# Two transformer blocks on one core: another order of ScalarE's steps in each expert, both gather halves evicted together, and the steps between router and first expert rearranged

## The chip, the cores and the metric

The kernel runs on one core of one Trainium2 chip. The metric is the device time of one execution in microseconds (us), start to end. PE is TensorE (matmuls), DVE is VectorE, ACT is ScalarE, POOL is GpSimd, SP is SyncE, which issues the loads of weights.

## The reference

A batch of one sequence of 256 tokens with 1024 features goes through two blocks in float32. The first block is a mixer (sliding-window attention with sinks, 8 heads of 64, beside gated linear attention), and then a mixture of 32 experts, of which each token takes its 4 best:

```
    logits = (h @ w_router).astype(jnp.float32) + b_router.astype(jnp.float32)
    top_v, top_i = lax.top_k(logits, TOP_K)
    gates = jax.nn.softmax(top_v, axis=-1)
...
        u = xb @ w_mlp1[e] + b_mlp1[e]
        x_glu = jnp.minimum(u[..., ::2], SWIGLU_LIMIT)
        x_lin = jnp.clip(u[..., 1::2], -SWIGLU_LIMIT, SWIGLU_LIMIT)
        a = x_glu * jax.nn.sigmoid(SWIGLU_ALPHA * x_glu) * (x_lin + 1)
        return a @ w_mlp2[e] + b_mlp2[e]
```

An expert goes from 1024 features to 2048 and, through `a` of 1024, back to 1024; a token's four results are added with their gates as weights.

The second block is a feed-forward part (2816 wide), a mixer of block attention (8 heads of 64) and spatial gating, and a second feed-forward part. All weights come from HBM once; the experts' are 384 MB.

## The kernel before

**Weights.** Every weight matrix is cut into chunks of 1 MB. `load_more` issues them on SP's queue in the order of use; a chunk is issued when the buffer that it takes has been released (`done`). In the expert stage there are 20 such buffers. An expert has 12 chunks: eight of `w_mlp1` (`m1`, k = 0 to 7) and four of `w_mlp2` (`m2`). They are released in fours: `m1` 0 to 3 after the branch at L1604, `m1` 4 to 7 after the branch at L1655, the `m2` four after the branch at L1672. All instructions stand in the order in which the code is written (`manual_schedule`), engine by engine.

**Router.** After the mixer, PE transposes the token rows and computes the router's logits (`pl`); DVE finds the four best, their one-hot rows `oh` and the counts `M`; PE makes positions from `M` (`pp`), DVE makes the selection `sel` of the first two experts. `x_hi` and `x_lo` are the rounded high part and the rest of the token rows: ACT copies `x_hi` (L1347), POOL subtracts `x_lo` (L1348).

**Gather.** Two experts are a group of 128 slots. `gather_rows` multiplies `sel` with `x_hi` and `x_lo` into two banks of 512 features, `gather_half` evicts one bank to `xr` on ACT (scaled by `yg`), PE transposes it four times into the same bank, and ACT and DVE take turns to write `xg`, features by slots, of both experts. There is one buffer `xr`, so the second eviction waits until the first half is transposed. The gather of the next group stands in the odd expert of a group, between the matmuls of that expert.

**An expert.** `up_start` writes the biases into two banks `u`; `up` multiplies `xg` with the eight `m1` chunks, of which the first half of the outputs (bank `u0`) ends earlier than the second. `glu` is four DVE steps and one ACT sigmoid `s` for each half and gives `a_sb`. Then comes the branch at L1655 (`more > 0`: the expert has over 64 tokens), `turn` (two transposes and ACT's copy to `aT`), the slot rows `pm`, and `down_q` over the four `m2` chunks into `yp`; before its second chunk the second half is turned. `rows_out` evicts `yp` (`yh`, `yl`), and `spread` adds it to the output banks `o_ps` during the next expert. `aT` has one buffer and shares it with `vx` of the branch. Before, the code reads:

```
            glu(us, a_sb, (0, 1))
            ax = P.tile([128, 1, 256], F32, name="ax", tag="sely", bufs=1)
            with tc.If(more > 0):
                nc.vector.tensor_tensor(vx, vx, up_more(range(4, KD)), op=OP.add)
                glu([vx], ax)
            ...
            pt = wps("apt")
            turn(a_sb, (0,), aT, pt)
```

**Attention.** `Attention.step` computes the scores of one pair of heads: for each head a matmul of 256 keys, one of 128 and the mask. A head has 64 features, so that the first head's matmuls use rows 0 to 63 of the array and the second's rows 64 to 127. There are four such steps in each block.

Of the kernel before, what the change touches and what calls it, by code (L numbers as in the profile page):

```python
# [10 lines left out]
F32 = mybir.dt.float32  # L11
# [4 lines left out]
AF = mybir.ActivationFunctionType  # L16
OP = mybir.AluOpType
# [7 lines left out]
CAP = 64  # L25
MORE = 32
# [20 lines left out]
def body(ctx: ExitStack, tc: tile.TileContext, I, out, dbg=None, n_experts=NE):  # L47
# [489 lines left out]
    class Attention:  # L537
# [8 lines left out]
        def step(self, i):  # L546
            pool, qT, kT = self.pool, self.qT, self.kT(i)
            ps = [self.bank("sc0"), self.bank("sc1")]
            for s in range(2):
                r = slice(64 * s, 64 * s + 64)  # L550
                nc.tensor.matmul(ps[s][:, 128:384], qT[r, i, 128:256], kT[r, :], start=True, stop=False,  # L551
                                 skip_group_check=True)
                nc.tensor.matmul(ps[s][:, 0:128], qT[r, i, 0:128], kT[r, 0:128], start=False, stop=False,
                                 skip_group_check=True)
                nc.tensor.matmul(ps[s][:, 0:384], ident_b, self.mask, start=False, stop=True, skip_group_check=True)
            yield
            S = pool.tile([128, 2, 384], F32, name="S", tag="S", bufs=2)
# [646 lines left out]
    with ExitStack() as ph:  # L1204
# [12 lines left out]
                                        qsl(b).to_broadcast([128, n, w]), op=OP.is_equal)  # L1217
            return sel

        def gather_rows(sel, w):  # L1220

            ps = []
            for q in range(2):
                p = wps("xrp")
                if q == 0:
                    for b in range(2):
                        nc.tensor.matmul(p[0:w, 0:1], sel[:, b].bitcast(F32), yt[:, b:b + 1], start=(b == 0),
                                         stop=(b == 1), skip_group_check=True)
                    yg = P.tile([128, 1], F32, name="yg", tag="yg", bufs=2)
                    nc.vector.tensor_copy(yg[0:w, :], p[0:w, 0:1])  # L1230
                    ps.append(yg)
                    first = p
                else:
                    for n, pn in ((1, p), (0, first)):
                        for b in range(2):
                            for x in (x_hi, x_lo):
                                nc.tensor.matmul(pn[0:w, :], sel[:, b], x[:, b, n * 512:(n + 1) * 512],  # L1237
                                                 start=(b == 0 and x is x_hi), stop=(b == 1 and x is x_lo),
                                                 skip_group_check=True)
                    ps += [p, first]  # L1240
            return ps

        def gather_half(ps, q, w, xgs):

            yg, p = ps[0], ps[1 + q]
            q = 1 - q
            xr = P.tile([128, 512], F32, name="xr", tag="yh", bufs=1)
            nc.scalar.activation(xr[0:w, :], p[0:w, :], AF.Copy, scale=yg[0:w, :])  # L1248
            for c in range(4):
                nc.tensor.transpose(p[:, c * w:(c + 1) * w], xr[0:w, c * 128:(c + 1) * 128], ident[0:w, 0:w])  # L1250
            for i, xg in enumerate(xgs):
                for c in range(4):
                    k = 4 * q + c
                    at = p[:, c * w + i * CAP:c * w + (i + 1) * CAP]
                    if c < 2:
                        nc.scalar.activation(xg[:, k, :], at, AF.Identity, scale=gs[:, 2, k:k + 1],  # L1256
                                             bias=modT[:, 24 + k:25 + k])
                    elif c == 2:
                        v = xg[:, k:k + 2, :]
                        at = p[:, c * w:4 * w].rearrange("p (c s) -> p c s", c=2)[:, :, i * CAP:(i + 1) * CAP]  # L1260
# [56 lines left out]

        x1 = xpool.tile([128, KD, T], F32, name="x1", tag="xb")
        pts = [acc("ht") for _ in range(4)]
        pl = wps("pl")  # L1320
        for h in range(2):
            for b in range(2):
# [16 lines left out]
                             stop=(b == 1), skip_group_check=True)  # L1339
        dump("x1T", x1)  # L1340

        x_hi = xpool.tile([128, 2, D], F32R, name="x_hi", tag="xb")
        x_lo = P.tile([128, 2, D], F32R, name="x_lo")
        for h in (1, 0):
            for b in range(2):
                cs = slice(h * 512, (h + 1) * 512)
                nc.scalar.activation(x_hi[:, b, cs], x_tok[:, b, cs], AF.Copy)  # L1347
                nc.gpsimd.tensor_tensor(x_lo[:, b, cs], x_tok[:, b, cs], x_hi[:, b, cs].bitcast(F32), op=OP.subtract)  # L1348
        slots.append((xpool, "xa", state["moe_end"] - 14))
        rt = P.tile([128, 2, NE], F32, name="rt", tag="aT")  # L1350
        for b in range(2):
            nc.vector.scalar_tensor_tensor(rt[:, b, :], pl[:, b * 32:(b + 1) * 32], yt[:, b:b + 1], lbias,
# [14 lines left out]
        for b in range(2):  # L1367
            with nc.allow_low_precision(reason="zeros and ones"):
# [11 lines left out]
        nc.vector.tensor_scalar(nit, pp[:, 64:96], float(MORE - 1 - CAP), None, op0=OP.add)  # L1380
        nc.vector.tensor_scalar(nit, nit, MORE.bit_length() - 1, None, op0=OP.arith_shift_right)
        nc.vector.tensor_scalar(nit, nit, 0.0, None, op0=OP.max)

# [4 lines left out]
        xg0 = group_tile(0)  # L1388
        w = group_size(0) * CAP
        xrs = gather_rows(sel0, w)  # L1390
        for h in range(2):
            gather_half(xrs, h, w, xg0)
        cur = sel0, xg0
# [12 lines left out]
        SW.close()  # L1406
        MW = ph.enter_context(ExitStack())
        banks["w"] = MW.enter_context(tc.tile_pool(name="psM", bufs=1, space=bass.MemoryType.PSUM))
        banks["tags"] = ["w0", "w1"]

        o_ps = [acc("moe_o") for _ in range(4)]
        for p in o_ps:

            nc.tensor.matmul(p, oh3[96:128, 0:1].to_broadcast([32, 128]), b13[96:128, 0:512], start=True, stop=False,
                             skip_group_check=True, tile_position=(96, 0))

        def o_part(b, dh, n):

            m = D // n
# [16 lines left out]
        def blocks(us, w):  # L1436
            n = 128 // w
            return [(us[i // n][w * (i % n):w * (i % n) + w, :], i, w * (i % n)) for i in range(4)]

        def up_start(us, w, e):  # L1440
            for u, i, c in blocks(us, w):
                nc.tensor.matmul(u, oh3[:, e:e + 1].to_broadcast([128, w]), b13[:, i * 512:(i + 1) * 512], start=True,
                                 stop=False, skip_group_check=True, tile_position=(0, c))

        def glu(us, a_sb, rs=(0,)):
            for r in rs:
# [117 lines left out]
        for e in range(n_experts):  # L1564
# [2 lines left out]
            sel, xg = cur  # L1567
            if look:
                nsel = group_select(gi + 1)
            us = [banks["w"].tile([128, 512], F32, name=f"u{i}", tag=f"u{i}") for i in range(2)]  # L1570

            def up(i, ks, us=us, xg=xg, e=e, j=j):
                for k in ks:
# [4 lines left out]
            up_start(us, CAP, e)  # L1578
            for k in range(3):
                up(0, (k,))  # L1580
                up(1, (k,))
# [26 lines left out]
                done(("m1", e, k))  # L1608
            if look:
                w = group_size(gi + 1) * CAP  # L1610
                xrs = gather_rows(nsel, w)
                nxg = group_tile(gi + 1)
                ahead = nsel, nxg

# [35 lines left out]
            a_sb = P.tile([128, 2, 256], F32, name="a_sb", tag="yl", bufs=1)  # L1650
            tg = P.tile([128, 2], F32, name="tg", tag="tg", bufs=1)
            sg = P.tile([128, T], F32R, name="sg", tag="sg", bufs=1)
            glu(us, a_sb, (0, 1))
            ax = P.tile([128, 1, 256], F32, name="ax", tag="sely", bufs=1)
            with tc.If(more > 0):  # L1655
                nc.vector.tensor_tensor(vx, vx, up_more(range(4, KD)), op=OP.add)
# [3 lines left out]
                done(("m1", e, k))  # L1660
            pt = wps("apt")
            turn(a_sb, (0,), aT, pt)
            pm = banks["w"].tile([128, 512], F32, name="pm", tag="u0")
            slots_of(e, sel[:, :, j], CAP, pm)
            slot_rows(pm, tg, sg)
# [397 lines left out]
```

## Time and profile before

| | us |
|---|---|
| median of 3 runs | 1793.35 (1787.22 to 1801.39) |
| the profiled execution | 1790.39 |
| its span, first to last instruction | 1788.7 |
| PE busy in the span | 1631.0 (91%) |
| DVE busy | 682.5 (38%) |
| ACT busy | 521.6 (29%) |

The experts' matmuls with `m1` chunks begin at 199.30 us of the span, and the last one with an `m2` chunk ends at 1202.0; the second block takes the rest. An expert takes from 26.4 to 50.6 us. The granted clock of TensorE is 0.969 of full over the span.

### The profile page before, as it was taken

How to read it: one execution, taken by the hardware profiler on the slowest of the kernel's cores; microseconds unless marked ns; L12 is line 12 of the kernel's file. 1: busy time of each engine (PE TensorE's matmuls, PEld its weight loads, DVE VectorE, ACT ScalarE, POOL GpSimd, SP SyncE). 2: the span in 40 equal slices, each digit the busy share in tenths (PEclk: the TensorE clock that was granted, in tenths of full speed). 3: DMA queues.
4: the chain of work that ended last, by engine and by line, in shares of the span. 5: the costliest groups of instructions: out<-in, count | busy, mean ns of one | idle time of the engine just before them, and what ended most of it. 6: DMA issues, size and time to landing. Idle time of an engine off the chain costs nothing. (4 is left out here: it accounts for less than half of the span.)

```text
span 1788.7 us, 25600 instructions
## 1 busy us (share of the span) xinstructions
PE 1631.0 (91%) x10067; PEld 996.7 (56%) x10067; DVE 682.5 (38%) x1424; ACT 521.6 (29%) x983; POOL 27.1 (2%) x43
## 2 busy tenths in 40 slices
PE   6998799999898798998989898888999999999997
PEld 3876333333333233333333333338999998999997
DVE  4656311211212112122121212217666775666666
ACT  2544211111011011111011111126444555554444
POOL 1000100000000000000000000100000000000000
PEclk8999899999899999999999999998999999999999
DMA  9987699799999999969999999973656653446552
GB/s 319 372 259 310 263 413 399 274 401 414 410 375 413 413 358 415 415 265 414 411 413 416 413 416 413 416 277 119 200 168 198 196 170 119 155 141 211 176 178 95
DMA packets 169755, 545.69 MB, mean 305 GB/s; under 512 B 11280, under 2 KB 90720, under 8 KB 133728
## 3 DMA queue, kind: packets, MB, share of 16 engines
q1 hardware_dynamic: 168304, 540.60, 79.0%
q8 instruction: 130, 2.13, 0.5%
q0 software_dynamic: 480, 1.58, 0.3%
q10 hardware_dynamic: 784, 0.92, 0.2%
q14 instruction: 57, 0.47, 0.1%
HBM read 542.01 MB, written 1.05 MB: 304 GB/s over the span
## 5 line engine op out<-in xcount | busy, mean ns | idle before, releaser
L1575 PE MATMUL u<-chunk,xg 128*64 128x512 f32 x2048 | 473.4, 604 | 2.7 <-PEq L1604 2.4
L1575 PEld LDWEIGHTS u<-chunk,xg 128*64 128x64 f32 x2048 | 156.2, 138 | 256.4 <-issue 247.0
L1477 PE MATMUL yp<-chunk,aT 128*64 128x512 f32 x1024 | 252.0, 636 | 48.4 <-ACT aT L1462 48.4
L448 DVE TENSOR_TENSOR ul<-chunk,uh 128x1024 fp32r<-128x1024 f32 x202 | 239.1, 1219 | 37.6 <-ACT uh L434 37.4
L434 ACT ACTIVATE uh<-chunk 128x1024 fp32r<-128x1024 f32 x202 | 205.2, 1049 | 59.5 <-DMA chunk<-in_ffn_w_up_dram 26.4
L310 PE MATMUL gu<-nhi,uh 128*128 128x256 f32 x704 | 200.1, 284 | 0.0
L310 PE MATMUL gu<-nhi,ul 128*128 128x256 f32 x704 | 199.4, 283 | 0.0
L310 PE MATMUL gu<-nlo,uh 128*128 128x256 f32 x704 | 199.4, 283 | 0.0
L1477 PEld LDWEIGHTS yp<-chunk,aT 128*64 128x64 f32 x1024 | 70.5, 143 | 174.3 <-issue 122.0
L310 PEld LDWEIGHTS gu<-nhi,uh 128*128 128x128 f32 x704 | 135.4, 192 | 1.2 <-issue 0.4
L310 PEld LDWEIGHTS gu<-nlo,uh 128*128 128x128 f32 x704 | 135.4, 192 | 0.9
L310 PEld LDWEIGHTS gu<-nhi,ul 128*128 128x128 f32 x704 | 135.4, 192 | 0.0
L1487 DVE SCALAR_TENSOR_TENSOR yl<-yp,tg,yh 128x512 fp32r<-128x512 f32 x32 | 24.0, 751 | 285.4 <-ACTq L1604 217.2
L1453 ACT ACTIVATE s<-g 128x256 f32<-128x256 f32 x66 | 27.5, 417 | 293.1 <-DVE g L1452 290.6
L1452 DVE TENSOR_SCALAR g<-u 128x256 f32<-128x256 f32 x64 | 27.1, 423 | 214.6 <-PE u L1575 212.8
L1486 ACT ACTIVATE yh<-yp,tg 128x512 fp32r<-128x512 f32 x32 | 22.0, 687 | 167.3 <-PEq L1672 150.4
L1248 ACT ACTIVATE xr<-xrp,yg 128x512 f32<-128x512 f32 x32 | 22.0, 686 | 145.1 <-PE xrp L1237 145.1
L1256 ACT ACTIVATE xg<-xrp,modT,gs 128x64 f32<-128x64 f32 x128 | 44.7, 399 | 64.6 <-PE xrp L1250 53.1
L1261 DVE TENSOR_TENSOR xg<-xrp,gs 128x128 f32<-128x128 f32 x64 | 18.7, 292 | 116.6 <-ACT xg L1256 116.6
L1142 DVE TENSOR_TENSOR gu<-gu,rs 128x512 f32<-128x512 f32 (+1 forms) x46 | 30.7, 667 | 80.7 <-PE gu L310 80.3
L1462 ACT ACTIVATE aT<-apt 128x256 f32<-128x256 f32 x64 | 24.5, 383 | 125.7 <-PE apt L297 93.6
L297 PEld LDWEIGHTS apt<-ident,a_sb 128*128 128x128 f32 x128 | 13.8, 149 | 77.9 <-issue 55.8
(472 smaller groups left out, 2402.4 us busy)
## 6 DMA issues: line engine op xcount, KB each, us to landing
chunk<-in_w_mlp_dram SPq DMA_DIRECT2D x384, 1024.0 KB, 9.5
chunk<-in_w_ada_dram SPq DMA_DIRECT2D x24, 1024.0 KB, 7.3
chunk<-in_ffn_w_gate_dram SPq DMA_DIRECT2D x22, 1024.0 KB, 5.4
chunk<-in_ffn_w_up_dram SPq DMA_DIRECT2D x22, 1024.0 KB, 7.9
chunk<-in_ffn_w_down_dram SPq DMA_DIRECT2D x22, 1024.0 KB, 5.8
chunk<-in_w_in_dram SPq DMA_DIRECT2D x17, 1024.0 KB, 5.2
chunk<-in_w_gate_dram SPq DMA_DIRECT2D x8, 1024.0 KB, 5.2
chunk<-in_w_out_dram SPq DMA_DIRECT2D x6, 1024.0 KB, 8.1
```

The lines of the kernel that those rows point to most:

```text
L310: nc.tensor.matmul(ps, a, b, start=first, stop=False, skip_group_check=True)
L434: nc.scalar.activation(hi if spec is None else spec(hi), view(raw(key)), AF.Copy)
L448: nc.vector.tensor_tensor(vl, view(raw(key)), vh.bitcast(F32), op=OP.subtract)
L1142: nc.vector.tensor_tensor(gu[:, a0:a1, :], p, rs[:, None, :].to_broadcast([128, a1 - a0, T]), op=OP.mult)
L1248: nc.scalar.activation(xr[0:w, :], p[0:w, :], AF.Copy, scale=yg[0:w, :])
L1256: nc.scalar.activation(xg[:, k, :], at, AF.Identity, scale=gs[:, 2, k:k + 1], bias=modT[:, 24 + k:25 + k])
L1452: nc.vector.tensor_scalar(g, uv[:, :, 0], 7.0, None, op0=OP.min)
L1453: nc.scalar.activation(s, g, AF.Sigmoid, scale=1.702)
L1462: nc.scalar.activation(aT[:, r * 256:(r + 1) * 256], pt[:, r * 256:(r + 1) * 256], AF.Copy)
L1477: nc.tensor.matmul(yp[w * d:w * d + w, 0:m], a, wt[:, o:o + m], start=(q + h == 0), stop=(q + h == 4), skip_group_check=True, tile_positio ...
L1487: nc.vector.scalar_tensor_tensor(yl, yp[:, 0:m], tg[:, 1:2], yh.bitcast(F32), op0=OP.mult, op1=OP.subtract)
L1575: nc.tensor.matmul(u, xg[j][:, k, :], raw(("m1", e, k))[:, n * 512:(n + 1) * 512], start=False, stop=(k == KD - 1), skip_group_check=True, ...
```

## The change

- In an expert the second half's `glu` stands behind the branch and behind the first half's `turn`. On ACT the order is sigmoid, copy to `aT`, sigmoid, copy, where it was two sigmoids and two copies.
- The gather evicts both banks one after the other (`gather_out`, two buffers `xr`), then transposes both; features 0 to 511 come first, and the `x_hi` matmuls of a bank stand ahead of its `x_lo` ones.
- `x_lo` is computed by DVE, after `yg` of the first group, where POOL computed it after each part of `x_hi`.
- The matmuls that open the output banks `o_ps` with zeros and the first expert's biases (`up_start`) stand ahead of the router's `pp`; the banks are laid out earlier for it. Four small DVE steps (`nit`, `nmax`, `q3`) move behind the first gather.
- The scores of a pair of heads alternate between the heads.

```
-            for s in range(2):
-                r = slice(64 * s, 64 * s + 64)
+            for s, r in enumerate(rows):
                 nc.tensor.matmul(ps[s][:, 128:384], qT[r, i, 128:256], kT[r, :], start=True, stop=False,
                                  skip_group_check=True)
+            for s, r in enumerate(rows):
                 nc.tensor.matmul(ps[s][:, 0:128], qT[r, i, 0:128], kT[r, 0:128], start=False, stop=False,
                                  skip_group_check=True)
+            for s in range(2):
                 nc.tensor.matmul(ps[s][:, 0:384], ident_b, self.mask, start=False, stop=True, skip_group_check=True)
...
+        def gather_out(ps, w):
+            xr = []
+            for q in range(2):
+                xr.append(P.tile([128, 512], F32, name="xr", tag="yl" if q else "yh", bufs=1))
+                nc.scalar.activation(xr[q][0:w, :], ps[1 + q][0:w, :], AF.Copy, scale=ps[0][0:w, :])
+            return ps[1:], xr
...
-                nc.gpsimd.tensor_tensor(x_lo[:, b, cs], x_tok[:, b, cs], x_hi[:, b, cs].bitcast(F32), op=OP.subtract)
...
+        def low_parts():
+            for h in range(2):
+                for b in range(2):
+                    cs = slice(h * 512, (h + 1) * 512)
+                    nc.vector.tensor_tensor(x_lo[:, b, cs], x_tok[:, b, cs], x_hi[:, b, cs].bitcast(F32),
+                                            op=OP.subtract)
+        xrs = gather_out(gather_rows(sel0, w, low_parts), w)
...
-            glu(us, a_sb, (0, 1))
+            glu(us, a_sb)
             ax = P.tile([128, 1, 256], F32, name="ax", tag="sely", bufs=1)
             with tc.If(more > 0):
...
             turn(a_sb, (0,), aT, pt)
+            glu(us, a_sb, (1,))
             pm = banks["w"].tile([128, 512], F32, name="pm", tag="u0")
```

ACT in an expert without a gather, before (L1655 is the branch, and the `s` inside it runs only when it is taken; `s` is the sigmoid's output):

```order
L1453 ACTIVATE s<-g 128x256 x2
L1655 COMPARE_AND_BRANCH
L1453 ACTIVATE s<-g 128x256
L1655 UNCONDITIONAL_BRANCH x2
L1462 ACTIVATE aT<-apt 128x256 x2
```

and with the change:

```order
L1475 ACTIVATE s<-g 128x256
L1678 COMPARE_AND_BRANCH
L1475 ACTIVATE s<-g 128x256
L1678 UNCONDITIONAL_BRANCH x2
L1484 ACTIVATE aT<-apt 128x256
L1475 ACTIVATE s<-g 128x256
L1484 ACTIVATE aT<-apt 128x256
```

The first copy to `aT` now stands ahead of the second half's sigmoid; DVE's four steps of that half moved behind its branch in the same way.

PE between the router's logits (`pl`) and the first expert's `m1` matmuls, before (`oh_71` picks the bias rows, `moe_o` are the output banks):

```order
L1338 MATMUL pl_1805<-fold,lpart 128x32 x2
...
L1375 MATMUL pp<-M,ones_b 128x32
L1227 MATMUL xrp<-rqy,sel 128x1 x2
...
L1250 MATMUL xrp<-ident,xr 128x128 x8
...
L1414 MATMUL moe_o<-b_70,oh_71 128x512
...
L1442 MATMUL u_1925<-b_70,oh_71 64x512
L1575 MATMUL u_1924<-chunk,xg 64x512 x2
```

and with the change:

```order
L1352 MATMUL pl_1809<-fold,lpart 128x32 x2
...
L1359 MATMUL moe_o<-b_70,oh_71 128x512
...
L1368 MATMUL u_1821<-b_70,oh_71 64x512
...
L1408 MATMUL pp<-M,ones_b 128x32
L1230 MATMUL xrp<-rqy,sel 128x1 x2
...
L1260 MATMUL xrp<-ident,xr 128x128 x8
L1597 MATMUL u_1820<-chunk,xg 64x512 x2
```

The eight bias matmuls moved from behind the gather's transposes to ahead of `pp`, so that the first `m1` matmul follows the transposes.

## Rows read from the trace of the kernel before

**Rows 1.** Groups by line over the whole span: x count, busy us, mean ns, idle

```profile
L1575 PEld LDWEIGHTS u<-chunk,xg 128*64 128x64 f32 x2048 | 156.2, 138 | 256.4 <-issue 247.0 <-DMA chunk<-in_w_mlp_dram 5.6 <-DMA chunk<-in_ffn_w_gate_dram 0.3
...
L448 DVE TENSOR_TENSOR ul<-chunk,uh 128x1024 fp32r<-128x1024 f32 x202 | 239.1, 1219 | 37.6 <-ACT uh L434 37.4
```

**Rows 2.** Stretches: length, busy by engine, granted clock, DMA share, GB/s

```profile
259.70:287.70 28.00, 25.79 (x124) 9.08 (x122) 4.39 (x11) 2.57 (x6) 0.00 (x0) 0.94 1.02 410
287.70:338.00 50.30, 45.55 (x344) 18.47 (x342) 12.38 (x42) 9.76 (x25) 0.00 (x0) 0.98 0.82 324
...
854.60:881.00 26.40, 24.20 (x122) 8.82 (x120) 4.39 (x11) 2.28 (x6) 0.00 (x0) 1.00 1.01 405
881.00:912.70 31.70, 28.15 (x142) 10.89 (x140) 7.19 (x22) 6.33 (x16) 0.00 (x0) 1.00 1.02 415
810.00:1180.00 370.00, 333.28 (x1651) 124.88 (x1649) 72.28 (x205) 53.68 (x124) 4.67 (x2) 1.00 1.02 414
```

**Rows 3.** PE's timeline in experts 24 and 2: start, us, count, idle before, releaser

```profile
979.36 7.09 PE L1575 MATMUL u<-chunk,xg 128*64 128x512 f32 x32 [0.16 <-PEq L1604]
986.75 0.41 PE L297 MATMUL apt<-ident,a_sb 128*128 128x128 f32 x2 [0.30 <-PEq L1655]
...
988.98 1.94 PE L1477 MATMUL yp<-chunk,aT 128*64 128x512 f32 x8 [1.49 <-ACT aT L1462]
...
277.71 3.20 PE L1477 MATMUL yp<-chunk,aT 128*64 128x512 f32 x8 [1.44 <-ACT aT L1462]
```

**Rows 4.** ACT's timeline in expert 24

```profile
988.54 0.38 ACT L1462 ACTIVATE aT<-apt 128x256 f32<-128x256 f32 x1 [1.12 <-DVEq L1655]
```

**Rows 5.** PE's timeline in expert 23, which gathers the next group

```profile
955.16 0.66 PE L1250 MATMUL xrp<-ident,xr 128*128 128x128 f32 x4 [0.56 <-ACT xr L1248]
...
960.11 0.41 PE L297 MATMUL apt<-ident,a_sb 128*128 128x128 f32 x2 [0.71 <-DVE a_sb L1456]
...
962.51 1.94 PE L1477 MATMUL yp<-chunk,aT 128*64 128x512 f32 x8 [1.66 <-ACT aT L1462]
```

**Rows 6.** PE's timeline between the router and expert 0

```profile
195.62 0.66 PE L1250 MATMUL xrp<-ident,xr 128*128 128x128 f32 x4 [2.43 <-ACT xr L1248]
196.21 1.80 PE L1414 MATMUL moe_o<-b,oh 32*128 32x512 bf16 x4
...
199.30 8.95 PE L1575 MATMUL u<-chunk,xg 128*64 128x512 f32 x32
```

**Rows 7.** DVE's timeline there: two of `oh`, and one of `og` later

```profile
183.70 2.64 DVE L1365 TENSOR_TENSOR oh<-iota_e,if 128x128 f32<-128x128 f32 x2
...
200.22 0.29 DVE L1404 TENSOR_TENSOR og<-oh,ex 128x128 f32<-128x128 f32 x1
```

**Rows 8.** POOL's timeline there

```profile
182.34 5.15 POOL L1348 TENSOR_TENSOR x_lo<-x_tok,x_hi 128x512 fp32r<-128x512 f32 x4 [2.96 <-ACT x_hi L1347]
```

**Rows 9.** SP's queue: issues of expert chunks from 127 to 348 us, and from 810.2

```profile
127.50 220.67 SPq L112 DMA_DIRECT2D chunk<-in_w_mlp_dram  x70
...
810.32 336.56 SPq L112 DMA_DIRECT2D chunk<-in_w_mlp_dram  x137
```

**Rows 10.** Time to landing of the single chunks issued at 785.4, 810.3, 1146.6

```profile
DMA to landing us min/median/max: 4.9/4.9/4.9
...
DMA to landing us min/median/max: 9.3/9.3/9.3
...
DMA to landing us min/median/max: 20.0/20.0/20.0
```

**Rows 11.** PE's timeline: scores of one pair in block two; spread in expert 24

```profile
1485.42 0.70 PE L551 MATMUL sc<-k,q 64*128 64x256 f32 x2
...
1486.54 0.70 PE L551 MATMUL sc<-k,q 64*128 64x256 f32 x2
...
976.13 0.73 PE L1505 MATMUL moe_o<-yh,sg 64*128 64x512 f32 x4
976.71 0.62 PE L1505 MATMUL moe_o<-yl,sg 64*128 64x512 f32 x4
```

More of the change, by code (lines that the diff above doesn't have):

```diff
@@ L548, in step @@
             ps = [self.bank("sc0"), self.bank("sc1")]
-            for s in range(2):
-                r = slice(64 * s, 64 * s + 64)
+            rows = [slice(64 * s, 64 * s + 64) for s in range(2)]
+            for s, r in enumerate(rows):
                 nc.tensor.matmul(ps[s][:, 128:384], qT[r, i, 128:256], kT[r, :], start=True, stop=False,
                                  skip_group_check=True)
+            for s, r in enumerate(rows):
                 nc.tensor.matmul(ps[s][:, 0:128], qT[r, i, 0:128], kT[r, 0:128], start=False, stop=False,
                                  skip_group_check=True)
+            for s in range(2):
                 nc.tensor.matmul(ps[s][:, 0:384], ident_b, self.mask, start=False, stop=True, skip_group_check=True)
@@ L1218, in select, with gather_rows @@
             return sel
-        def gather_rows(sel, w):
+        def gather_rows(sel, w, between=None):
             ps = []
@@ L1231, in gather_rows @@
                     ps.append(yg)
+                    if between is not None:
+                        between()
                     first = p
                 else:
-                    for n, pn in ((1, p), (0, first)):
-                        for b in range(2):
-                            for x in (x_hi, x_lo):
+                    for n, pn in ((0, p), (1, first)):
+                        for x in (x_hi, x_lo):
+                            for b in range(2):
                                 nc.tensor.matmul(pn[0:w, :], sel[:, b], x[:, b, n * 512:(n + 1) * 512],
@@ L1241, in gather_rows @@
             return ps
+        def gather_out(ps, w):
[4 more added lines that the diff above has]
+            return ps[1:], xr
         def gather_half(ps, q, w, xgs):
[L1245 to L1248, printed above, removed]
+            p, xr = ps[0][q], ps[1][q]
             for c in range(4):
@@ L1319, in body @@
         pts = [acc("ht") for _ in range(4)]
+        SW.close()
+        MW = ph.enter_context(ExitStack())
+        banks["w"] = MW.enter_context(tc.tile_pool(name="psM", bufs=1, space=bass.MemoryType.PSUM))
+        banks["tags"] = ["w0", "w1"]
         pl = wps("pl")
@@ L1340, in body, with blocks, up_start, up_banks @@
         dump("x1T", x1)
+        o_ps = [acc("moe_o") for _ in range(4)]
+        for p in o_ps:
+            nc.tensor.matmul(p, oh3[96:128, 0:1].to_broadcast([32, 128]), b13[96:128, 0:512], start=True, stop=False,
+                             skip_group_check=True, tile_position=(96, 0))
+        def blocks(us, w):
+            n = 128 // w
+            return [(us[i // n][w * (i % n):w * (i % n) + w, :], i, w * (i % n)) for i in range(4)]
+        def up_start(us, w, e):
+            for u, i, c in blocks(us, w):
+                nc.tensor.matmul(u, oh3[:, e:e + 1].to_broadcast([128, w]), b13[:, i * 512:(i + 1) * 512], start=True,
+                                 stop=False, skip_group_check=True, tile_position=(0, c))
+        def up_banks():
+            return [banks["w"].tile([128, 512], F32, name=f"u{i}", tag=f"u{i}") for i in range(2)]
+        us0 = up_banks()
+        up_start(us0, CAP, 0)
         x_hi = xpool.tile([128, 2, D], F32R, name="x_hi", tag="xb")
         x_lo = P.tile([128, 2, D], F32R, name="x_lo")
-        for h in (1, 0):
+        for h in range(2):
             for b in range(2):
@@ L1347, in body @@
                 nc.scalar.activation(x_hi[:, b, cs], x_tok[:, b, cs], AF.Copy)
-                nc.gpsimd.tensor_tensor(x_lo[:, b, cs], x_tok[:, b, cs], x_hi[:, b, cs].bitcast(F32), op=OP.subtract)
-        slots.append((xpool, "xa", state["moe_end"] - 14))
         rt = P.tile([128, 2, NE], F32, name="rt", tag="aT")
@@ L1380, in body @@
         nc.vector.tensor_scalar(nit, pp[:, 64:96], float(MORE - 1 - CAP), None, op0=OP.add)
+        def low_parts():
+            for h in range(2):
+                for b in range(2):
+                    cs = slice(h * 512, (h + 1) * 512)
+                    nc.vector.tensor_tensor(x_lo[:, b, cs], x_tok[:, b, cs], x_hi[:, b, cs].bitcast(F32),
+                                            op=OP.subtract)
+        xg0 = group_tile(0)
+        w = group_size(0) * CAP
+        xrs = gather_out(gather_rows(sel0, w, low_parts), w)
+        slots.append((xpool, "xa", state["moe_end"] - 14))
+        for h in range(2):
+            gather_half(xrs, h, w, xg0)
+        cur = sel0, xg0
         nc.vector.tensor_scalar(nit, nit, MORE.bit_length() - 1, None, op0=OP.arith_shift_right)
@@ L1387, in body @@
         nc.vector.tensor_scalar(q3, q1, -float(CAP), None, op0=OP.add)
[L1388 to L1393, printed above, removed]
         ex = P.tile([128, 2, 4], F32, name="ex")
@@ L1405, in body @@
             nc.vector.tensor_reduce(gt2[:, b, :, 1], og[:, b].rearrange("p k e -> p e k"), axis=AX.X, op=OP.add)
[L1406 to L1415, printed above, removed]
         def o_part(b, dh, n):
@@ L1434, in slot_rows @@
             nc.vector.tensor_scalar(sg, iota_t, pm[:, 0:1], None, op0=OP.is_equal)
[L1436 to L1443, printed above, removed]
         def glu(us, a_sb, rs=(0,)):
@@ L1569, in body @@
                 nsel = group_select(gi + 1)
-            us = [banks["w"].tile([128, 512], F32, name=f"u{i}", tag=f"u{i}") for i in range(2)]
+            us = up_banks() if e else us0
             def up(i, ks, us=us, xg=xg, e=e, j=j):
@@ L1576, in up @@
                                          start=False, stop=(k == KD - 1), skip_group_check=True, tile_position=(0, c))
-            up_start(us, CAP, e)
+            if e:
+                up_start(us, CAP, e)
             for k in range(3):
@@ L1610, in body @@
                 w = group_size(gi + 1) * CAP
-                xrs = gather_rows(nsel, w)
+                xrs = gather_out(gather_rows(nsel, w), w)
                 nxg = group_tile(gi + 1)
```

## The prediction

> **What bounds the kernel now.** I read the groups by line first, then the stretches, then the timelines of one expert, and SP's queue last. In [rows 1] PE's loads of `xg` for the `m1` matmuls waited for a weight chunk for 5.6 us in all 32 experts, while `yp` waited 1.49 and 1.66 us for ACT's copy `aT` in the two experts of [rows 3, 5]: so the experts, 1003 of 1789 us, are paced by PE's own chain, and some 1.5 us an expert of it is that copy. But the loads are close behind. In the stretch from 810 to 1180 us of [rows 2] the DMA engines were busy throughout (share 1.02, 414 GB/s). The same pace from [rows 9, 10]: the chunk issued at 810.3 landed after 9.3, at 819.6; the one issued at 1146.6, 136 chunks later (the last of the 137), after 20.0, at 1166.6: 347.0 / 136 = 2.55 us a chunk, 30.6 an expert. An undisturbed expert without a gather (20) takes 26.4 and one with it (21) 31.7 [rows 2], a mean of 29.05. PE is thus already 1.5 us an expert faster than the loads, and lives on what the 20 buffers hold after a slow expert: expert 3, which has over 64 tokens, took 50.3 with the DMA share at 0.82 [rows 2], since all buffers were full. Whatever the change takes off PE's chain, the loads decide how much of it is kept.
>
> **An expert without a gather** (expert 24, [rows 3, 4]). The matmuls into `u` end at 986.45, the branch costs 0.30, the transposes `apt` start at 986.75, and `yp` at 988.98: 2.23 us. In between ACT was free from 987.42, but `aT` started at 988.54, released by DVE's branch at L1655, which stands behind both halves of `glu`. With the change DVE reaches the branch after the first half, two microseconds before PE's transposes, and ACT's copy needs the transposes alone: 0.41 + 0.38 for the copy + some 0.10 for two handoffs = 0.89. Saved: 2.23 - 0.89 = **1.34**. What is late next is the second half: copy 0.38, sigmoid 0.42, and two DVE steps of 0.42 give some 1.75 us with handoffs, counted from the start of the copy (987.18 now). PE wants the second turn when the first quarter of `yp` is through, 1.9 after its start [rows 3], so 2.3 us after that point. Margin 0.5: taken as no wait. The other DVE steps (`tg`, `sg`) are wanted only at the end of `yp`.
>
> **An expert with a gather** [rows 5]. The second transposes waited 0.56 for the single buffer `xr`; both evictions now end long before. The chain behind (four `xg` writes in turns, then the first `glu`) moves with them, and `apt`, which waited 0.71 for `a_sb`, starts 0.56 earlier. Then `apt` to `yp` shrinks from 2.40 to 0.89: 1.51. Saved: **2.07**. The order of `x_hi` and `x_lo` costs PE nothing there, both being old. In the two experts that take the branch (3 and 17) DVE passes it only after the extra matmuls; saved 0, bounds -0.6 to +0.6 (the second half now starts later, the eviction is earlier).
>
> **Router to expert 0** [rows 6 to 8]. Three pieces stood on the chain. `oh` took 2.64 for two while POOL ran `x_lo` (182.34 for 5.15); one of the same shape took 0.29 later: saved 2.06. The second transposes waited 2.43 for the second eviction: about 2.3 saved, as it now follows the first by a matmul group. The eight bias matmuls, 196.21 to 199.30, go into the time in which PE waits for `M`: saved 3.09. Against it stand the four `x_lo` steps on DVE behind `yg`: half of 1219 ns [rows 1] to 0.69 each, 2.4 to 2.8 us. The gather, eight matmuls of 0.43 after `yg`, needs its last low part near the end as well, so PE loses 0.1 (bounds 0 to 2.8). Sum **7.4**, bounds 4.6 to 9. The softmax steps pushed back have the 12 us of `m1` as cover; `nit` is wanted at the first branch, 9 us later.
>
> **Scores** [rows 11]. One head's scores take 1.12, two heads 2.0 to the next matmul. The two heads use different rows of the array, and the trace has such pairs in `spread`: four matmuls of 512 columns on 64 rows take 0.58, 0.145 each, against 0.222 for the `m1` matmuls (7.09 / 32). An fp32 matmul is two instructions here, written head after head, so I expect half the overlap: some 0.4 a step (bounds 0 and 0.85). In block two that is **1.6** at full weight, since PE is dense there; in block one I count half, 0.8. The Trainium skill ("TensorEngine Tiling (Array Packing)", Key Properties) says that tiles run matmuls in parallel and that a change of mode drains the array. By that rule a step would save the whole 0.85, block two 3.4; no row shows this order.
>
> **The clock.** In the stretch of expert 2 (28.00 us, clock 0.94) against expert 20 (26.40, clock 1.00) [rows 2], a fall to 1.2 GHz costs 1.6 us. It came at the start of `yp`, whose first eight took 3.20 there against 1.94 in expert 24 [rows 3], after the 2.2 us in which PE had two transposes and eight tiny matmuls. Nine of the experts 1 to 19 have such a stretch (0.90 to 0.95, two of them with two falls' worth). With that pause at 0.9 I expect most to go: 16 us on PE's chain, bounds 0 to 16; experts 1 and 2 (3.2) lie before expert 3.
>
> **The sum.** PE's chain alone: 7.4 + 0.8, 17 experts without a gather x 1.34 = 22.8, 13 with one x 2.07 = 26.9, and up to 16 for the clock: 58 to 74. Now the loads. After expert 3 all buffers were full; the 69th chunk was issued at 347.3 (the 70 issues of [rows 9] end at 348.2, the last two half a microsecond apart), when expert 4 released its first four. From there on, PE at some 28.2 us an expert against 30.6 (13 experts, 31 us gained, with 51 us in the buffers) never leaves the queue without a free buffer again, not even in expert 17, so the loads run without a pause to the end. What moves the 69th issue is only what is saved before it: 7.4 + 0.8 + 1.34 x 2 + 2.07 + 3.2 = 16.2. It goes out at 331.1, lands 5 us later (the 4.9 of [rows 10]), and the last of the other 315 at 336.1 + 315 x 2.55 = 1139.4. The last eight `yp` matmuls follow: 2.0, so 1141.4, where they ended at 1202.0: a gain of 60.6. The loads set the end, some 13 us short of PE's chain. For a rest of full buffers around experts 12 and 13 (where a read of `nit` holds PE) I take 3.5 off: **57**. Block two adds 1.6, and the first feed-forward chunks, which now land right behind, may cost 1.6. The total is 57. The profiled execution was 1790.39, so 1733.4; its median is 2.96 higher, and the forecast for the median is 1793.35 - 57 = **1736**.
>
> **Rivals.**
> 1. *The falls of the clock stay, or the savings come out a quarter smaller.* Then PE's chain, 58 or 45 to 50, sets the time, full buffers return at expert 17, and from there the loads keep the end from moving by more than the 15.6 us between the last landing (1166.6 + 7 x 2.55 = 1184.5) and its use at 1200.1. Gain 42 to 52: 1741 to 1751.
> 2. *The wait comes back at the second turn.* If branch, sigmoid and handoffs take 3.0 instead of 1.75, PE waits 0.7 in every expert: 22 us off the chain, gain about 33: 1760. For it: ACT took 1.12 beside a branch in [rows 4]. Against: nothing but the sigmoid stands between the two copies.
> 3. *The copy stays behind a branch.* If `aT` were still released late, only 7.4, 0.8, 1.6 and 0.56 x 13 remain: 17 us, 1776. The order of ACT speaks against it.
> 4. *The buffers never fill,* not even in expert 3. Then the loads run on from the first release, 199.30 + 8.95 = 208.3 [rows 6], 200.1 after the gains there: 364 chunks, the last landing at 200.1 + 5 + 363 x 2.55 = 1130.8. Gain up to 69, 1724.
> 5. *Slower: the clock falls where PE now waits for chunks.* In the last seven experts PE is some 20 us ahead of the loads and pauses before each chunk. A fall costs 1.6; 14 of them, two an expert, cost 22 and are mostly paid out of the pauses. It decides from 57 / 1.6 = 36 falls more than now; if PE stayed at 1.2 GHz through experts 22 to 31, 24 us of matmuls would become 48, 17 over the loads' pace: 170 - 57 = 113 slower, 1906. The Trainium skill ("TensorE: Matmul & The Clock Gate", HAM oscillation) tells of a kernel whose DMA waits threw the clock back at each tile. In this trace the clock rose again within the same expert (0.94 in [rows 2]), and the pauses would end as soon as PE is the slower.
>
> **How the numbers follow.** Forecast 0.48 (1728 to 1741), rival 1 0.25, rival 2 0.09, rival 3 0.05, rival 4 0.08, rival 5 0.03, and 0.02 for other. The range reaches from rival 4's side, with 3 to 4 us for an unhidden scores gain, to rival 2: 1722 to 1760. One per cent, 18 us, is about what can be told from no change. All but rivals 3 (half of it within 18 us) and 5 are beyond it: faster 0.93, same 0.04, slower 0.03.
>
> **What would show it.** Each step: `aT` starting under 0.1 us after the transposes, and `yp` 0.9 after their start; the second `xrp` transposes without a wait; `oh` at 0.29 each and the first `m1` matmul near 192; a pair's scores in 1.2 to 1.6; fewer than five falls of the clock between 250 and 850. The loads' share near 1.0 from 340 to 1140 without a gap at expert 17, and PE waiting for chunks only in the last experts. I am wrong if the DMA share still drops in expert 17 (then rival 1), or if `apt` waits for the second `a_sb`.

## The result, and the profile after

The changed kernel takes **1726.2 us** (median of 4 runs, 1724.81 to 1727.09), the kernel before 1795.63 (median of 4, 1787.22 to 1801.39): a ratio of 0.9616 with a 95% interval of 0.9575 to 0.9657, 69 us. The forecast was 1736, its range 1722 to 1760. The profiled execution took 1726.06 with a span of 1724.3, against 1790.39 and 1788.7.

The experts come first, as stretches (length, busy time by engine, granted clock, DMA share, GB/s); they answer to [rows 2].

```profile
190.00:210.00 20.00, 19.20 (x96) 6.77 (x94) 7.64 (x28) 5.75 (x12) 0.00 (x0) 1.00 0.76 293
...
268.10:317.90 49.80, 44.94 (x344) 18.11 (x342) 11.94 (x41) 9.89 (x25) 0.00 (x0) 1.00 0.96 391
310.00:330.00 20.00, 18.58 (x135) 7.81 (x136) 1.87 (x6) 1.55 (x3) 0.00 (x0) 0.91 0.60 228
...
795.10:820.30 25.20, 24.23 (x123) 8.80 (x120) 4.30 (x11) 2.22 (x6) 0.00 (x0) 1.00 1.02 415
820.30:849.90 29.60, 28.08 (x142) 10.90 (x140) 7.10 (x22) 6.29 (x16) 0.00 (x0) 1.00 1.02 414
345.00:1140.00 795.00, 734.86 (x3722) 273.60 (x3718) 158.20 (x464) 117.44 (x276) 5.96 (x4) 0.99 1.01 413
```

Experts 20 and 21 take 25.2 and 29.6 (26.4 and 31.7 in [rows 2]), and expert 3 takes 49.8 (50.3). From 345 to 1140 us the DMA engines never rest: share 1.01 over 795 us, expert 17 within it. In the kernel before they had 0.99 at 400 GB/s from 350 to 1180. Their last rests are the two at 190 and 310 us, where all buffers are full.

PE's timeline in expert 24, then ACT's (start, us, count, idle before and its releaser):

```profile
913.28 7.09 PE L1597 MATMUL u<-chunk,xg 128*64 128x512 f32 x32 [0.16 <-PEq L1627]
920.67 0.41 PE L297 MATMUL apt<-ident,a_sb 128*128 128x128 f32 x2 [0.30 <-PEq L1678]
921.00 0.40 PE L1459 MATMUL pm<-gt,sel 128*64 128x2 f32 x8
921.60 1.94 PE L1499 MATMUL yp<-chunk,aT 128*64 128x512 f32 x8 [0.20 <-ACT aT L1484]
923.47 0.44 PE L297 MATMUL apt<-ident,a_sb 128*128 128x128 f32 x2
```

```profile
921.17 0.38 ACT L1484 ACTIVATE aT<-apt 128x256 f32<-128x256 f32 x1 [3.32 <-DVE a_sb L1476]
921.45 0.41 ACT L1475 ACTIVATE s<-g 128x256 f32<-128x256 f32 x1
923.95 0.38 ACT L1484 ACTIVATE aT<-apt 128x256 f32<-128x256 f32 x1 [2.09 <-PE apt L297]
```

The copy starts 0.09 after the transposes end, `yp` 0.93 after their start (2.23 in [rows 3]), and the second turn follows the first eight `yp` without a wait. In expert 23 the second `xrp` transposes do not wait any more (0.56 in [rows 5]); PE's timeline:

```profile
890.55 0.66 PE L1260 MATMUL xrp<-ident,xr 128*128 128x128 f32 x4
891.14 3.65 PE L1597 MATMUL u<-chunk,xg 128*64 128x512 f32 x16
895.51 0.41 PE L297 MATMUL apt<-ident,a_sb 128*128 128x128 f32 x2 [0.72 <-DVEq L1678]
896.44 1.94 PE L1499 MATMUL yp<-chunk,aT 128*64 128x512 f32 x8 [0.19 <-ACT aT L1484]
```

Between router and expert 0, PE and then DVE ([rows 6, 7]):

```profile
187.59 0.80 PE L1260 MATMUL xrp<-ident,xr 128*128 128x128 f32 x4
188.57 0.66 PE L1260 MATMUL xrp<-ident,xr 128*128 128x128 f32 x4 [0.18 <-ACT xr L1253]
189.16 6.23 PE L1597 MATMUL u<-chunk,xg 128*64 128x512 f32 x28
```

```profile
181.06 0.17 DVE L1394 CAST if<-i 128x16 f32<-128x16 uint32 x1
181.27 0.49 DVE L1398 TENSOR_TENSOR oh<-iota_e,if 128x128 f32<-128x128 f32 x2
```

The experts start at 189.16 instead of 199.30. In the last seven PE does what it hardly did before, when its loads for the `m1` matmuls waited 5.6 us in all [rows 1]: it waits for chunks, 15.1 us in its matmuls alone. PE in experts 26 and 31, and then a pair's scores in block two ([rows 11]):

```profile
973.24 1.08 PE L1597 MATMUL u<-chunk,xg 128*64 128x512 f32 x4 [1.41 <-DMA chunk<-in_w_mlp_dram]
975.74 4.51 PE L1597 MATMUL u<-chunk,xg 128*64 128x512 f32 x20 [1.42 <-DMA chunk<-in_w_mlp_dram]
...
1141.05 1.94 PE L1499 MATMUL yp<-chunk,aT 128*64 128x512 f32 x8 [1.20 <-DMA chunk<-in_w_mlp_dram]
...
1426.55 0.70 PE L552 MATMUL sc<-k,q 64*128 64x256 f32 x4
1427.08 0.39 PE L555 MATMUL sc<-k,q 64*128 64x128 f32 x4
1427.40 0.50 PE L558 MATMUL sc<-mask_b,ident_b 128*128 128x384 bf16 x2
1427.61 0.41 PE L310 MATMUL gt<-nhi,uh 128*128 128x256 f32 x1
```

Two heads' scores of 256 keys now take 0.70, as long as one head's did, and it is 1.06 us from the pair's start to the next matmul (1427.61) instead of 2.00 (1485.42 in [rows 11] to this line of the kernel before):

```profile
1487.42 0.41 PE L310 MATMUL gt<-nhi,uh 128*128 128x256 f32 x1
```

**Where the 64.3 us of the span came from:** the experts' start 10.1 earlier, the experts themselves 48.9 shorter (their end at 1143.0 instead of 1202.0), block two 5.3 shorter.

### The profile page after: what moved, and what is told of

It reads as the page before. It is cut to its first block, busy times and chain, and to the rows that moved or that the text cites. A ratio compares the mean times of both kernels' runs of the same rounds, so it can differ in the third digit from the quotient of the medians.

```text
span 1724.3 us, 25602 instructions
## 1 busy us (share of the span) xinstructions
PE 1606.3 (93%) x10067; PEld 982.3 (57%) x10067; DVE 679.9 (39%) x1428; ACT 520.0 (30%) x983; POOL 21.9 (1%) x39
## 5 line engine op out<-in xcount | busy, mean ns | idle before, releaser
L1597 PE MATMUL u<-chunk,xg 128*64 128x512 f32 x2048 | 475.8, 604 | 16.7 <-DMA chunk<-in_w_mlp_dram 13.9
L1597 PEld LDWEIGHTS u<-chunk,xg 128*64 128x64 f32 x2048 | 152.7, 138 | 275.9 <-issue 235.6
L1499 PE MATMUL yp<-chunk,aT 128*64 128x512 f32 x1024 | 235.8, 602 | 9.5 <-ACT aT L1484 8.1
L1148 ACT ACTIVATE fs<-gu 128x256 f32<-128x256 f32 x44 | 18.4, 418 | 122.9 <-DVE gu L1145 122.9
```

What stands on the lines that cost most here:

```text
L1499: nc.tensor.matmul(yp[w * d:w * d + w, 0:m], a, wt[:, o:o + m], start=(q + h == 0), stop=(q + h == 4), skip_group_check=True, tile_positio ...
```

## The experiments

Two theories were to be told apart. **L**, the prediction's: PE's chain sets the time up to the issue of the 69th expert chunk, and from there the loads run without a rest and set the end of the experts. **P**: PE's chain sets all of it. One table tells most of it; the times are of each kernel's profiled execution, the median is of its runs.

| kernel | first `m1` matmul | 69th issue | end of the experts | from 69th issue to end | span | median |
|---|---|---|---|---|---|---|
| before | 199.3 | 347.3 | 1202.0 | 854.7 | 1788.7 | 1795.6 |
| before_again | 199.2 | 348.5 | 1198.0 | 849.5 | 1785.8 | 1791.4 |
| changed | 189.2 | 327.9 | 1143.0 | **815.1** | 1724.3 | 1726.2 |
| changed_again | 191.1 | 328.2 | 1143.2 | **815.0** | 1726.0 | 1727.4 |
| glu_order_alone | 200.2 | 339.6 | 1154.5 | **814.9** | 1741.1 | 1744.0 |
| glu_order_undone | 189.4 | 331.4 | 1183.4 | 852.0 | 1766.2 | 1769.1 |
| one_xr_in_loop | 189.4 | 327.6 | 1142.7 | **815.2** | 1723.9 | 1728.6 |
| work_added_early | 189.5 | 331.8 | 1146.8 | **815.0** | 1729.6 | 1733.5 |
| work_added_late | 189.3 | 327.9 | 1143.0 | **815.1** | 1726.0 | 1728.1 |
| scores_undone | 192.1 | 330.9 | 1145.9 | **815.0** | 1732.6 | 1735.2 |
| x_lo_on_pool | 192.3 | 331.0 | 1145.9 | **814.9** | 1728.7 | 1730.4 |
| biases_late | 190.1 | 327.2 | 1142.2 | **815.0** | 1725.6 | 1728.0 |
| one_xr_first | 194.3 | 335.1 | 1150.1 | **815.0** | 1733.2 | 1733.3 |
| half_loads | 190.2 | 327.2 | 1120.1 | 792.9 | 1703.2 | 1704.1 |

Ten of the fourteen rows, with PE's work up to 10 us apart behind that issue, have 815.0 from it to the end, within 0.2. Where the span is compared below, it is with `changed_again`, for a reason that its own paragraph gives.

**glu_order_alone.** The kernel before, with this part alone:

```
-            glu(us, a_sb, (0, 1))
+            glu(us, a_sb)
...
             turn(a_sb, (0,), aT, pt)
+            glu(us, a_sb, (1,))
```

> The kernel before, with only the new order of the second half's sigmoid and copies in an expert. Theory L (PE's chain until the 69th chunk of the experts is issued, then the loads): the steps before that issue save 1.25 + 1.45 + 1.25 = 4.0, and up to 3.2 for two falls of the clock, so that issue comes at 340 to 343 instead of 347.3; with the 815 us that the changed kernel took from there to the last yp matmul, the expert stage ends at 1155 to 1158, 44 to 47 earlier: 1744 to 1748 in a profiled run. Theory P (PE's chain sets all of it): 17 x 1.25 + 13 x 1.45 = 40, and 16 for the falls, makes 56: 1734. If the falls stay, both give 40: 1750. Falls of the clock between 250 and 850 us: fewer than five if the pause ahead of yp causes them, ten if not.

The result is 1743.96, a ratio of 0.9718 (0.9652 to 0.9783). That is theory L, since the 815 us hold here too. The part alone brings 50 of the 69 us. The clock record has 2 falls between 250 and 850 us, where the kernel before has 13 in one profile and 9 in another (`before_again`).

**glu_order_undone.** The changed kernel with `glu(us, a_sb, (0, 1))` back in its place.

> The changed kernel, with both halves' glu back ahead of the branch. PE is slow again and sets the time: its start at 189.2 stays, an odd expert keeps the 0.56 of the gather, so the stage ends at 189.2 + 1002.7 - 13 x 0.56 = 1184.6, 42 later than the changed kernel: 1766 to 1770. If the changed order were worth its full 56 on top of the other parts (theory P): 1782. Falls of the clock between 250 and 850: ten or more if the pause ahead of yp causes them.

The result is 1769.13, a ratio of 0.9854 (0.9785 to 0.9923); the experts ended at 1183.4, 1.2 from the working. An expert without a gather takes 26.40 again, no matmul with an `m1` chunk waits for a load, and 11 falls of the clock are back. Stretch, and PE at one of the falls:

```profile
331.00:1180.00 849.00, 766.16 (x3798) 285.73 (x3798) 164.24 (x474) 122.46 (x281) 5.94 (x4) 0.96 0.98 396
...
908.19 3.13 PE L1499 MATMUL yp<-chunk,aT 128*64 128x512 f32 x8 [1.44 <-ACT aT L1484]
```

Again the wait of 1.44 stands ahead of `yp`, and eight matmuls take 3.13 instead of 1.94. The order of ACT is worth 43 here and 50 alone, and the other parts 25 without it and 18 with it: the parts do not add up, because from the 69th issue on one limit caps them all.

**one_xr_in_loop.** In the loop only, one eviction buffer again:

```
-                xrs = gather_out(gather_rows(nsel, w), w)
+                xrs = gather_rows(nsel, w)
```

with the eviction to a single `xr` at the head of `gather_half`.

> The changed kernel, with a single buffer xr for the gathers inside the experts (the first gather keeps two). PE waits 0.56 more in each odd expert. Theory P: 14 or 15 x 0.56 = 8 slower than the changed kernel, 1734. Theory L: only expert 1 lies before the 69th issue, so 0.6 slower (0 to 1.5), 1727, with PE's waits for chunks in the last experts shorter by the other 7.

An odd expert takes 30.23 instead of 29.66, so PE did lose 0.57 in each, some 8 us in all; the experts ended at 1142.7. That is theory L. The median, 1728.6, is 1.3 above that of `changed_again`, and the four times spread over 3.7; so inside the experts the two buffers are worth nothing that can be told from the spread.

**work_added_early** and **work_added_late.** In experts 0 to 2, or 18 to 23, ahead of the first `turn`:

```
+            for _ in range(8 if 18 <= e < 24 else 0):
+                for h in range(2):
+                    transpose(pt[:, h * 128:(h + 1) * 128], a_sb[:, 0, h * 128:(h + 1) * 128])
```

> The changed kernel, with 16 more transposes of a_sb (0.165 us each, into the same bank as before) ahead of the turn in experts 0, 1 and 2: 2.6 us more on PE in each, 7.9 in all, and all of it ahead of the 69th issue. Theory L: that issue and the end move by as much, 7 to 8 slower: 1733 to 1735. Theory P says the same. A third, that the front of the stage has slack (PE's first experts wait for nothing but the buffers were filled before), 0 to 3.

> The changed kernel, with the same 16 transposes in experts 18 to 23: 6 x 2.6 = 15.8 us more on PE, behind the 69th issue. PE waited for chunks for some 19 us in the last seven experts. Theory L: 0 to 2 slower, 1726 to 1728, with those waits down to 3 to 5 us. Theory P: 15.8 slower, 1742.

The 16 transposes cost 1.75 each time and not 2.6 (18 of them take 2.16 in a row, 2 take 0.41), so the size was off in both. Late, PE did 10.5 us more and the experts ended at 1143.0, the span was 1726.0: **nothing**. PE's matmuls waited 8.6 us for chunks instead of 15.1 (3 to 5 were expected, with the larger size), and the fall of the clock at 1034.5 us of the changed kernel's profile did not come. Early, 5.2 more: the 69th issue and the end moved by 3.6 against `changed_again`, which had itself started 1.6 later. Against `changed` they moved by 3.9 and 3.8 only, because there the clock fell once, at 317.7 us, ahead of the issue. From the first `m1` matmul to the 69th issue three profiles with the changed order and no such fall take 137.1 (`changed_again`, `biases_late`, `half_loads`), four with one fall take 138.7 (`changed`, `work_added_late`, `scores_undone`, `x_lo_on_pool`), and `work_added_early`, without a fall, takes 142.3: 5.2 more. The medians of the two runs, 1733.5 and 1728.1, lie 5.4 apart. The same work is paid in full in front of the issue and free behind it.

**half_loads.** From expert 8 on each chunk brings only its first half (the edit to `load_more`; `raw` gives that half twice):

```
+            if half[0] <= i < half[1]:
+                src = chunks[i][0][1]
+                nc.sync.dma_start(t[:, :1024], src[:, :1024] if len(src.shape) == 2 else src[:, 0, :])
```

> The changed kernel, in which from expert 8 on a chunk loads only the first half of its columns and the matmuls use that half twice (the second half of these weights is left out, so the output is another one). PE's work stays. Theory L: only PE's waits for chunks go, 18 us by the periods of the last seven experts (1.2, 3.8, 1.7, 7.1, 0.1, 3.6 and 0.7 over 29.66 or 25.16), so the experts end at about 1125 instead of 1143.0: 1706 to 1710, with no wait for a chunk left. Rival: the waits stand where PE would have waited anyway, within 3 us of 1726. If traffic slows PE's own matmuls, more than 20 us faster, with periods under 25.16.

The result is 1704.07, with the experts' end at 1120.1, 22.9 earlier and a little more than the 18 expected: expert 31 had waited for 3.7 and not 0.7, and this execution was 1.7 ahead at expert 24 already. PE's own matmuls were no faster (29.66 and 25.16 an expert) at 207 GB/s than at 413, so the traffic had not slowed them. Groups by line over the span (count, busy us, mean ns, idle before), and the last stretch of experts:

```profile
L1612 PE MATMUL u<-chunk,xg 128*64 128x512 f32 x2048 | 469.7, 600 | 2.9 <-PEq L1642 2.7
...
929.95:1120.00 190.05, 181.06 (x906) 68.80 (x902) 37.36 (x107) 28.24 (x66) 5.94 (x4) 1.00 0.62 207
```

No wait for a chunk is left in the group (13.9 us of 16.7 in the changed kernel). This is PE's chain by itself, about 23 us short of the loads.

**scores_undone.** One head's matmuls after the other's, as in the `-` lines of the diff.

> The changed kernel, with one head's scores after the other's again. By the steps of the trace (0.85 a step in block two, some 0.5 in block one): 3.4 + 2.1 = 5.5 slower, 1731 to 1732. By the prediction's half overlap: 2.4, 1728 to 1729. The faster matmuls of the mixer's end in block two (113.3 ns each, 117.8 before, 384 of them, 1.6 us) should stay with the changed kernel's if they have nothing to do with the scores; if they come with them, 1733.

The span is 1732.6, 6.6 more: 2.7 at the end of the experts and 3.9 in block two. A step costs 0.95 to 0.97 there, more than both guesses. The Trainium skill ("TensorEngine Tiling (Array Packing)", Key Properties) says that different tiles run their matmuls in parallel; the pair of [rows 11] turned into 0.70 for both agrees, and the prediction's half overlap does not.

**x_lo_on_pool.** The four subtractions back on POOL, behind each `x_hi`.

> The changed kernel, with the four low parts back on POOL, each behind its high part; the order of the matmuls stays. If POOL's subtractions slow DVE's steps of oh beside them (2.64 us for two in the kernel before, 0.49 in the changed one), the first m1 matmul starts 2 us later, at 191.3, and the end moves as much: 1728. Rival: DVE's own steps behind yg cost as much as they save: within 0.5 of 189.2. Upper bound, if the gather also waits for the last low part: 4 us.

The first `m1` matmul came at 192.3, 3.2 and 1.2 later than in the two profiles of the changed kernel, and the end of the experts 2.9 and 2.7 later. The clock was at half from 173.5 to 190.5 here and from 173.9 to 190.9 in `changed_again`, so the second comparison is the one at the same clock: 1.2, or 1.6 counted from the transposes ahead of the router, which came 0.4 earlier here. At the end of the experts 1.6 of the 2.7 is a fall of the clock at 320.2 that `changed_again` does not have. DVE's timeline:

```profile
181.43 1.03 DVE L1395 CAST if<-i 128x16 f32<-128x16 uint32 x1
182.49 2.63 DVE L1399 TENSOR_TENSOR oh<-iota_e,if 128x128 f32<-128x128 f32 x2
185.04 0.63 DVE L1403 TENSOR_REDUCE M<-oh 128x32 bf16<-128x128 f32 x2
```

While POOL ran (179.87 to 184.97) `oh` took 2.63 for 0.49, and the conversion to `if` 1.03 for 0.17: 3.0 in all on DVE. The start does not gain all of it, since DVE's four low parts then stand ahead of the gather: from its first `x_hi` matmul to the transposes it takes 3.90 in `changed_again` and 3.33 here. The Trainium skill ("GPSIMD Engine Reference", Specifications) says that POOL shares SBUF interfaces with VectorE, and that operations with two SBUF inputs contend; `oh`, which has two, agrees; the conversion has one input.

**one_xr_first.** One buffer `xr` in the first gather alone.

> The changed kernel, with a single buffer xr in the first gather only. The prediction gave the second eviction's wait 2.3 us. The second eviction would start after the first transposes instead of at 187.83: by the steps of the trace 188.3 + 0.7 + handoff = 189.1 against 188.57 for the second transposes, 0.6 later, 1727. By the prediction's 2.3: 1728.5.

My 0.6 was wrong: the experts ended 6.9 later than in `changed_again`. PE, then ACT:

```profile
193.28 1.12 PE L1265 MATMUL xrp<-ident,xr 128*128 128x128 f32 x4 [2.43 <-ACT xr L1261]
```

```profile
190.89 0.70 ACT L1271 ACTIVATE xg<-xrp,modT,gs 128x64 f32<-128x64 f32 x2 [1.87 <-PE xrp L1265]
191.95 0.70 ACT L1271 ACTIVATE xg<-xrp,modT,gs 128x64 f32<-128x64 f32 x2 [0.36 <-DVE xg L1276]
192.55 0.69 ACT L1261 ACTIVATE xr<-xrp,yg 128x512 f32<-128x512 f32 x1
```

The second eviction stands on ACT behind the first half's four `xg` writes, which I had left out, and PE waits the 2.43 of [rows 6] to the hundredth. The rest is the clock, at half from 174.6 to 198.5 in this profile (until 190.9 in `changed_again`) and once more at 324.8.

**biases_late.** The zeros and first biases behind the first gather again.

> The changed kernel, with the eight matmuls of zeros and first biases behind the first gather again. They took 3.1 us in the kernel before; the first m1 matmul starts 2.5 to 3.1 later, near 192, and the end moves as much: 1729. Rival: PE would then wait at the first expert for xg (ACT and DVE write it from 188.4 to 192.5), which hides them: 0 to 1.

The eight matmuls took 1.41 (188.69 to 190.10) and not 3.1, and the experts ended at 1142.2, earlier than in both profiles of the changed kernel. Counted from the first transposes ahead of the router, the first `m1` matmul came after 17.7 us, against 16.2 to 17.2 in the six other profiles with the changed order there whose clock was at half for 7 to 10 us. So the edit is worth 0.4 to 1.4 at the start, less than the 2 us by which the start differs between executions; at the end of the experts it cannot be told.

**before_again** and **changed_again.** Both kernels as they are.

> The kernel before once more, for a second profile: its four times spread over 14 us, those of the changed kernel over 2. If falls of the clock in the expert stage make that spread (1.6 us each, all on the path), then the time differs from 1790.4 by 1.6 us for each fall more or less than the 13 between 250 and 850 us, and the undisturbed experts take 26.40 and 31.72 again. Rival: the loads or the second block differ, at the same number of falls.

The profiled execution took 1787.62, 2.8 less, and the experts ended at 1198.0, 4.0 earlier than in the first profile, with undisturbed experts at 26.40 and 31.72 again. The falls between 250 and 850 us are 9 for 13, which by 1.6 each would be 6.4; up to 1150 us they are 11 for 13, which would be 3.2. So the window of the expectation was too short, and over the whole stage the count fits. Of thirteen other executions of the kernel before the two fastest, 1786.96 and 1787.20, have mean clocks of 0.968 and 0.971, the two slowest, 1804.24 and 1806.89, have 0.960 and 0.958.

> The changed kernel once more. In its first profile and in that of one_xr_in_loop the 384 matmuls of br and o in block two came every 113.3 ns, in the nine other profiles every 117.8, at the same granted clock: 1.6 us. If that is chance of an execution, this one has 117.8 more likely than not, the times lie at 1726 to 1728, and the differences of the other experiments shrink by up to 1.6. Rival: it belongs to this code, then 113.3 again and a median of 1726. The expert stage ends at 1143 again, within 1, by theory L, since it needs only the 69th issue at 327 to 328.

The result is 1727.35 (1724.61 to 1727.72, 6 runs) at a clock of 0.979 or 0.980 in all, a ratio of 0.9623 (0.9589 to 0.9656). The experts ended at 1143.2, as expected. Its `br` matmuls have the slower pace. The same form in the first profile of the changed kernel, and here (ns min/median/max):

```profile
L310 PE MATMUL br<-ath,ul x32: 276/276/281, 1478.6 to 1498.7; 128*128 128x256 f32 x32
```

```profile
L310 PE MATMUL br<-ath,ul x32: 281/281/282, 1478.6 to 1499.5; 128*128 128x256 f32 x32
```

So 1.6 of the 64.3 us between the first two profiles belong to an execution and not to the change.

No kernel here has a lower median than the changed one at the same work. By the table an earlier 69th issue would bring it; none of these edits brings one beyond what executions of the changed kernel differ by. Two parts of the change were not run alone: the order of the `x_hi` and `x_lo` matmuls, and the four small DVE steps.

## Why the prediction was right, and where its sizes were off

**The bound, right.** The loads took over at the 69th issue, as the sum had it: forecast 331.1, measured 327.9; forecast end 1141.4, measured 1143.0. The 3.5 us taken off for full buffers at experts 12 and 13 did not occur (a read at expert 12 held PE for 7.2 us as before, but behind the issue). Against that the loads ran at (815.1 - 5 - 2) / 315 = 2.565 us a chunk instead of 2.55, which is 4.8 over 315 chunks. 59.0 came out where 57 was forecast: 3.2 more ahead of the 69th issue and 3.5 not lost, less 4.8. That these nearly cancel is luck; that the loads set the end is not.

**PE's terms, right.** 1.24 and 2.06 an expert for 1.34 and 2.07, and no wait at the second turn. Most falls of the clock went: 4 for 13 between 250 and 850 us, 0.99 for 0.97 over the stretch. That they hang on the pause ahead of `yp` is shown by the pair of glu runs, 2 without it and 11 with it. (The prediction counted nine of the experts 1 to 19 with a stretch at 0.90 to 0.95; the stretches show ten, and one more at 0.85. The sum does not turn on it.)

**Router and first scores, 8.2 forecast, 10.1 measured** (8.2 in `changed_again`). The parts differ from the forecast: for `x_lo` 3.0 on DVE (2.06; the conversion to `if` was slowed too), of which 1.2 to 1.6 reached the first `m1` matmul at the same clock; for the second eviction 2.25, from a wait of 2.43 to one of 0.18 (2.3); for the biases 0.4 to 1.4 (3.09, a row taken at 1.2 GHz); and some 2.5 for the scores (0.8). They add up to 6.4 to 7.8. What the rest is stays open; the clock in this stretch differs from one execution to the next.

**Block two, 0 forecast, 5.3 measured.** The scores term was forecast at less than half its size, 1.6 for 3.8; the rest is the matmul pace. The 1.6 that the feed-forward's first chunks were to cost did not come: between the end of the experts and the first scores the lead stayed at 59.

**The step that made the forecast 10 us high** is these 5.3, 2.0 in the experts, and the last one: the profiled execution lay 2.96 below the median, and I carried that distance over. In the kernel before the falls of the clock lie on the path, and its executions spread over 12 to 20 us in a series. In the changed one PE's lead over the loads swallows those behind the 69th issue (one ahead of it still cost 1.6, see `work_added_early`); its executions spread over 2 to 3 us, and the median is within 0.2 of the profiled execution.

**The rivals.** Rivals 1 to 3 fell with the rows of expert 24 and the clock. Rival 4 gave 1724, close to what was measured, but not by its mechanism: the buffers did fill in expert 3, between 310 and 330 us (share 0.60). Rival 5's pauses came, and the clock fell once and twice in the last seven experts of the two profiles: PE waited 1.4 at a time between groups of four matmuls, and mostly went on at 2.4 GHz. In `half_loads`, without these waits, the clock did not fall from 740 to 1125 us, so a few falls do come with them, paid out of the pauses.

## What to carry to other kernels

Where a stream of loads is nearly as slow as the compute that it feeds, find the issue from which the stream never rests again: what is saved ahead of it counts in full, what is saved behind it counts until compute is the faster, and then not at all, for any part. Test it by adding work on either side of that point; it costs one run each, and a constant time from that issue to the end over several kernels, together with an end that comes earlier when the loads are halved, is strong evidence. A wait that lets the clock fall costs twice (here 1.44 us, and then 3.13 for eight matmuls instead of 1.94), and a kernel that such falls make uneven becomes even once something else bounds it.

## What the runs showed of the hardware that I had not expected

At the same granted clock of 1.00, a stretch of 384 matmuls of 256 columns runs at 113.3 or at 117.8 ns each, one or the other through the whole stretch: the faster in 2 of 14 profiles, and both occur with the same code. No run here tells why. POOL's subtraction slowed not only DVE's operation with two inputs but a conversion of 16 columns sixfold. And the clock at the experts' start is a matter of the execution: last at half until 188.0 in one profile of the changed kernel and until 190.9 in the other.
